# Prompt tokens read a second time channel by channel: the two front norms of a streaming encoder layer without transposes, and the first value products on unscaled channels

## The chip, the cores and the metric

The kernel runs on one core of one Trainium2 chip. The metric is device microseconds of one execution. A core has five engines that run their own instruction streams in order: TensorE (PE in the profile, with its weight loads as PEld), VectorE (DVE), ScalarE (ACT), GpSimd (POOL) and SyncE (SP, which here only issues DMAs). They wait for each other by semaphores.

## The reference

One layer is computed for 2048 prompt tokens and 32 sample tokens, with 1024 channels. What matters here is its start; everything behind it is unchanged.

```python
def rmsnorm(x, g):
    xf = x.astype(jnp.float32)
    y = xf * lax.rsqrt(jnp.mean(xf * xf, axis=-1, keepdims=True) + EPS)
    return (y * g.astype(jnp.float32)).astype(x.dtype)

def layer(x, pool_hist, n_valid, S0, g_pre_mix, w_in, ...):
    h = rmsnorm(x, g_pre_mix)
    z = h @ w_in
    u, zq, zf, zi, zg = jnp.split(z, [...], axis=-1)   # 512 columns each
    ...                      # pooling mixer on u, HGRN2 recurrence on q, f, i, g
    y_mix = jnp.concatenate([y_pool, y_hg], axis=-1) @ w_out
    x = x + rmsnorm(y_mix, g_post_mix)
    h2 = rmsnorm(x, g_pre_ffn)
    f = (jax.nn.silu(h2 @ w_gate) * (h2 @ w_up)) @ w_down
    return x + rmsnorm(f, g_post_ffn), ...
```

The norm's root belongs to a token, its gain g to a channel. The columns zi are the "values" of the recurrence: values = h @ w_in[:, 1536:2048].

## The kernel before

**Halves and stages.** The prompt is worked in two halves A and B of 1024 tokens, B together with the sample tokens. Each half goes through the same stages: front (norm, channels onto partitions), values, four heads (products f, q, g and the recurrence), four pooling groups, output projection, second norm, gate and up. At the end one down projection serves both halves. Half B's front starts while half A's last gate/up products run (`gate_up(S, on_last)` calls it eleven steps before its end).

**Precision.** Every large product is made of three products of rounded f32 values: an operand is split into a high part (a copy that rounds, on ACT) and a low part (operand minus high part, on DVE), and high x high, high x low and low x high are summed in PSUM. `split` does that for weights (tiles whw, wlw or whi, wlo), and hThi, hTlo hold the normed activations.

**The front.** `front_norm(S, tg)` treats a group of 512 tokens (tg 0 or 1). It loads four tiles xt of 128 tokens x 1024 channels, sums their squares on ACT (`sumsq`, tile junk), forms the roots on POOL (`rstd_of`), scales the tiles on DVE, and `to_channels` transposes them on PE into PSUM banks tps, 128x128 at a time, 32 transposes per group. Out of PSUM, ACT writes hThi with the gain as its scale, and DVE writes hTlo. At the program's start the first 256 tokens go ahead of the rest, and the vectors of gains (tile rows) are transposed by PE into vec.

**The values.** `values(S, tg)` takes eight rows of w_in in pairs and makes, for four token tiles and each channel row k, three products 128x512 into four PSUM banks (vps). In half A the first two pairs of tiles are worked apart, since their channels come at different times. Then come the heads. `head_products` makes f for tokens 0 to 511 and 512 to 1023, then q for both, then g.

**Order.** PE's order is the order in which the program is written; generator tasks (`Task`, `poll`) are stepped in between by a counted time of PE. The other engines' orders, SP's queue among them, are made by a scheduler. Weights come through `Stream`: `want` lists the loads, `ahead(n)` issues loads two items beyond n and splits the items up to n, `take` hands out the next. Large SBUF tiles come from a pool of 39 buffers (UP), tiles of 512 columns from one of 22 (TP), PSUM from two pools of four banks (MM for the large products, AX for everything else).

Of the kernel before, what the change touches and what calls it, by code (L numbers as in the profile page):

```python
# [16 lines left out]
P = 128  # L17
D = 1024
# [25 lines left out]
C_END = C_I4 + NS  # L44
# [29 lines left out]
def body(tc, ins, outs, cst):  # L74
    nc = tc.nc
    ctx = ExitStack()
    with ctx:
# [28 lines left out]
        x_first = []  # L106
        rows = t2("rows", [32, P])
        nc.vector.memset(rows, 0.0)
        for i in range(2):
            xt = ztile("xt", [P, D])  # L110
            nc.sync.dma_start(out=xt, in_=ins["x_prompt"][0, i * P:(i + 1) * P, :])
            x_first.append((xt, P))
            if i == 0:
                nc.sync.dma_start(out=cons, in_=cst)
            else:
                for ap, r0, n in ((ins["g_pre_mix"], 0, 8), (ins["g_pre_ffn"], 8, 8), (ins["pool_scale"], 16, 4),
                                  (ins["lb_logits"], 20, 8), (ins["g_hg_norm"], 28, 1)):
                    nc.sync.dma_start(out=rows[r0:r0 + n, :], in_=ap.rearrange("a (k p) -> (a k) p", p=P))
        ident = cons[:, C_ID:C_ID + P]
        x_p = ins["x_prompt"][0]  # L120
        x_s = ins["x_sample"][0]
        w_in = ins["w_in"][0]
# [5 lines left out]
        vec = CP.tile([P, 32], F32, name="vec")  # L128
        vps = axbank("vps")
        nc.tensor.transpose(vps[:, 0:32], rows, ident[0:32, 0:32])  # L130
        nc.vector.tensor_copy(vec, vps[:, 0:32])
# [16 lines left out]
        nc.gpsimd.memset(nhalf, -0.5)  # L148
        wpool = CP.tile([P, 4, P], F32, name="wpool")
# [88 lines left out]
        def raw_rows2(w, k, c0):  # L238
            raw = ztile("wrow", [P, 2 * 512])
            nc.sync.dma_start(out=raw.rearrange("p (k c) -> p k c", c=512),  # L240
                              in_=w[k * P:(k + 2) * P, c0:c0 + 512].rearrange("(k p) c -> p k c", p=P))
            return raw
# [11 lines left out]

        def ahead(n):
            its = Stream.items
            while Stream.nraw < min(n + LOOKRAW, len(its)):
                its[Stream.nraw] = its[Stream.nraw]()
                Stream.nraw += 1
# [43 lines left out]

        tcB = [0]

        def to_channels(tiles, dst, gcol, col0, seen=None, which=()):
            n = P * len(tiles)
            per = 512 // n
            for k0 in range(0, KD, per):
                ps = axbank("tps")  # L310
                for kk in range(per):
                    for i, xn in enumerate(tiles):
                        c = kk * n + i * P
                        nc.tensor.transpose(ps[:, c:c + P], xn[:, (k0 + kk) * P:(k0 + kk + 1) * P], ident)
                        tick(107)
                for kk in range(per):
                    k = k0 + kk
                    src = ps[:, kk * n:(kk + 1) * n]
                    hi, lo = dst[k]
                    nc.scalar.activation(hi[:, col0:col0 + n], src, AF.Copy, scale=gcol[:, k:k + 1])  # L320
                    nc.vector.scalar_tensor_tensor(lo[:, col0:col0 + n], src, gcol[:, k:k + 1],
                                                   hi[:, col0:col0 + n].bitcast(F32), ALU.mult, ALU.subtract)
                if seen is not None:
                    for i in which:
                        seen[i] = k0 + per
                yield (700.0 if seen is None and tcB[0] else 400.0) * per
# [95 lines left out]
        def make_half(B):  # L422
            S = Half()
            S.B = B
            S.T = TMAX if B else HALF
            S.tok0 = HALF if B else 0
            S.blocks = [(0, 512), (512, 1024)]
            return S


        def front_norm(S, tg):
            def channels():
                if S.hT is None:
                    S.hT = [(xtile(f"hThi{k}"), xtile(f"hTlo{k}")) for k in range(KD)]
                    if S.B:
                        S.hsr = SP.tile([P, KD, NS], F32, tag="hs", name="hsr", bufs=1)
                        S.ysr = SP.tile([P, KD, NS], F32, tag="ysr", name="ysr", bufs=1)

            early = not S.B and tg == 0
            xs = list(x_first) if early else []  # L440
            if early:
                ahead(0)
            for i in range(len(xs), 4):
                xt = ztile("xt", [P, D])
                r0 = S.tok0 + (tg * 4 + i) * P
                nc.sync.dma_start(out=xt, in_=x_p[r0:r0 + P, :])
                xs.append((xt, P))
            if S.B and tg == 1:
                xq = ztile("xts", [NS, D])
                nc.sync.dma_start(out=xq, in_=x_s)  # L450
                xs.append((xq, NS))
            yield 1000.0 if S.B else 0.0
            if early:
                channels()
                for a in (0, 2):
                    for xt, r in xs[a:a + 2]:
                        st = new_stat()
                        sumsq(xt, r, st[0:r, 0:1])
                        nc.vector.tensor_scalar(xt, xt, rstd_of(st, r, eng=nc.vector), None, ALU.mult)
                    yield 2000.0  # L460
                    yield from to_channels([x for x, _ in xs[a:a + 2]], S.hT, g_pre, a * P, S.seen[tg], (a // 2,))
                return
            rs = []
            for xt, r in xs:
                st = new_stat()
                sumsq(xt, r, st[0:r, 0:1])
                rs.append(rstd_of(st, r))
            for (xt, r), q in zip(xs, rs):
                nc.vector.tensor_scalar(xt, xt, q, None, ALU.mult)
            xq = xs[4][0] if len(xs) > 4 else None  # L470
            xs = [x for x, _ in xs[:4]]
            yield 8000.0 if S.B else 6000.0
            channels()
            yield from to_channels(xs, S.hT, g_pre, tg * 512, S.seen[tg], (0, 1))
            if xq is not None:
# [3 lines left out]
        def front_loads(S):  # L479
            for tg in range(2):  # L480
                for k in range(0, KD, 2):
                    want(lambda k=k: raw_rows2(w_in, k, COL_I), 1 if S.B or tg else 2)
# [10 lines left out]
        def values(S, tg):  # L493
            va, vb = ztile("va", [P, 2, 512]), ztile("vb", [P, 2, 512])
            S.vt += [va[:, 0], va[:, 1], vb[:, 0], vb[:, 1]]
            smp = S.B and tg == 1
            pss = [mmbank("vps") for _ in range(4)]
            sps = axbank("vsps") if smp else None
            four = Four(sps, KD)
            early = not S.B and tg == 0  # L500
            ws = {}
            steps = [(k, (0, 1, 2, 3)) for k in range(0, KD, 2)]
            if early:
                steps[0:2] = [(0, (0, 1)), (2, (0, 1)), (0, (2, 3)), (2, (2, 3))]
            for k, tiles in steps:
                if k not in ws:
                    ws[k] = take(1 if early else 2)
# [1063 lines left out]
```

## Time and profile before

| what | us |
|---|---|
| median of 3 runs (lowest to highest) | 2188.99 (2187.97 to 2190.52) |
| the profiled execution | 2187.68 |
| its span | 2185.9 |
| PE idle in the span | 42.2 |
| first transposes of xt | 9.1 |
| first value product | 14.34 |
| head 0's first product | 70.67 |
| first transposes of half B | 818.3 |
| its values begin | 841.5 |

The span runs from the first to the last instruction that the profiler records. Busy shares are of the span. A matmul's duration overlaps with that of the next, so on PE the step between two starts is what one costs. Durations of a group are means of one instruction in ns. The rows in the chapter on the prediction are copied from the profile's views as they are.

### The profile page before, as it was taken

How to read it: one execution, taken by the hardware profiler on the slowest of the kernel's cores; microseconds unless marked ns; L12 is line 12 of the kernel's file. 1: busy time of each engine (PE TensorE's matmuls, PEld its weight loads, DVE VectorE, ACT ScalarE, POOL GpSimd, SP SyncE). 2: the span in 40 equal slices, each digit the busy share in tenths (PEclk: the TensorE clock that was granted, in tenths of full speed). 3: DMA queues.
4: the chain of work that ended last, by engine and by line, in shares of the span. 5: the costliest groups of instructions: out<-in, count | busy, mean ns of one | idle time of the engine just before them, and what ended most of it. 6: DMA issues, size and time to landing. Idle time of an engine off the chain costs nothing.

```text
span 2185.9 us, 34308 instructions
## 1 busy us (share of the span) xinstructions
PE 2143.7 (98%) x13293; PEld 1712.5 (78%) x13293; DVE 1414.3 (65%) x2309; ACT 817.5 (37%) x1586; POOL 282.4 (13%) x383
## 2 busy tenths in 40 slices
PE   7999999999999999999999999999999999999996
PEld 5878878788888888777777778888888777877785
DVE  6356665697776778365574687766666756566585
ACT  6233234554444456132323564444444521011032
POOL 1033201100000001023220120000000210110033
PEclk9999999999999999999999999999999999999999
DMA  6110043425555558111014524544454797777789
GB/s 221 39 31 21 21 145 131 149 82 169 162 148 151 155 164 268 43 44 34 15 32 146 180 86 125 159 141 140 135 145 140 228 327 200 220 223 206 203 226 308
DMA packets 385179, 315.13 MB, mean 144 GB/s; under 512 B 15701, under 2 KB 318058, under 8 KB 385017
## 3 DMA queue, kind: packets, MB, share of 16 engines
q1 hardware_dynamic: 382856, 305.34, 46.0%
q0 software_dynamic: 2016, 7.34, 1.7%
q8 instruction: 105, 1.72, 0.3%
q14 instruction: 58, 0.47, 0.1%
q10 hardware_dynamic: 144, 0.26, 0.0%
HBM read 214.51 MB, written 98.37 MB: 143 GB/s over the span
## 4 chain that ended last, share of the span: by engine, by line
PE 43%; DVE 3%; DMA 2%; ACT 1%; POOL 1%; issue 0%; SPq 0%; DVEq 0%; POOLq 0%; ACTq 0%
PE gx L184 10%; PE dx L184 10%; PE gy L184 6%; PE dy L184 5%; PE ops L184 4%; PE dz L184 2%; PE gz L184 2%; PE mmb L184 1%; DMA hst<-hdTrue 1%; PE gsps L184 1%; DVE acc L1360 1%; PE gw L184 1%; PE sacc L184 0%; PE zps L184 0%; PE pps L184 0%
## 5 line engine op out<-in xcount | busy, mean ns | idle before, releaser
L184 PE MATMUL gx<-fhi,wf 128*128 128x512 f32 x1376 | 448.5, 394 | 0.0
L184 PEld LDWEIGHTS gx<-fhi,wf 128*128 128x128 f32 x1376 | 258.7, 188 | 59.2 <-issue 1.0
L184 PE MATMUL gx<-flo,wf 128*128 128x512 f32 x688 | 270.1, 393 | 0.0
L184 PE MATMUL gy<-fhi,wf 128*128 128x512 f32 x704 | 234.0, 394 | 0.0
L184 PE MATMUL mmb<-hThi,whi 128*128 128x512 f32 x512 | 219.0, 428 | 0.0
L184 PE MATMUL dx<-dhi,hst 128*128 128x512 f32 x640 | 213.5, 394 | 0.5 <-DVE acc L1360 0.4
L184 PE MATMUL mmb<-hThi,wlo 128*128 128x512 f32 x512 | 201.4, 393 | 0.0
L184 PE MATMUL mmb<-hTlo,whi 128*128 128x512 f32 x512 | 201.2, 393 | 0.0
L1360 DVE TENSOR_TENSOR acc<-dx,acc 128x512 f32<-128x512 f32 x168 | 115.2, 689 | 77.9 <-PE dx L184 77.3
L1094 DVE TENSOR_TENSOR wf<-s,wf 128x512 fp32r<-128x512 f32 x176 | 120.5, 688 | 66.1 <-ACT wf L1089 63.5
L184 PEld LDWEIGHTS gy<-fhi,wf 128*128 128x128 f32 x704 | 132.3, 188 | 30.6 <-issue 0.5
L184 PEld LDWEIGHTS gx<-flo,wf 128*128 128x128 f32 x688 | 129.6, 188 | 28.3
L1089 ACT CAST wf<-s 128x512 fp32r<-128x512 f32 x176 | 108.4, 621 | 105.4 <-PE gy L184 34.7
L184 PEld LDWEIGHTS dx<-dhi,hst 128*128 128x128 f32 x640 | 120.8, 189 | 32.2 <-issue 3.6
L184 PE MATMUL gy<-flo,wf 128*128 128x512 f32 x352 | 138.2, 392 | 0.0
L184 PE MATMUL dx<-dlo,hst 128*128 128x512 f32 x320 | 125.9, 394 | 0.0
L1094 DVE TENSOR_TENSOR wf<-wraw,wf 128x512 fp32r<-128x512 f32 x132 | 89.7, 687 | 50.9 <-ACT wf L1089 50.8
L184 PE MATMUL dy<-dhi,hst 128*128 128x512 f32 x320 | 113.1, 394 | 4.8 <-DMA hst<-hdTrue 4.4
L184 PEld LDWEIGHTS mmb<-hThi,whi 128*128 128x128 f32 x512 | 96.3, 188 | 25.0 <-issue 6.4
L1089 ACT CAST wf<-wraw 128x512 fp32r<-128x512 f32 x132 | 80.9, 620 | 88.3 <-PE gz L184 23.8
L184 PEld LDWEIGHTS mmb<-hThi,wlo 128*128 128x128 f32 x512 | 96.1, 188 | 22.3
L184 PEld LDWEIGHTS mmb<-hTlo,whi 128*128 128x128 f32 x512 | 96.7, 189 | 18.3 <-issue 2.6
(312 smaller groups left out, 4115.1 us busy)
## 6 DMA issues: line engine op xcount, KB each, us to landing
hst<-hdFalse SPq DMA_DIRECT2D x140, 256.0 KB, 2.9
hst<-hdTrue SPq DMA_DIRECT2D x140, 256.0 KB, 3.4
wraw<-in_w_gate_dram SPq DMA_DIRECT2D x50, 512.0 KB, 4.0
wraw<-in_w_up_dram SPq DMA_DIRECT2D x50, 512.0 KB, 3.9
hdFalse<-hhi SPq DMA_DIRECT2D x77, 256.0 KB, 2.6
hdFalse<-hlo SPq DMA_DIRECT2D x77, 256.0 KB, 2.5
hdTrue<-hhi SPq DMA_DIRECT2D x77, 256.0 KB, 2.4
hdTrue<-hlo SPq DMA_DIRECT2D x77, 256.0 KB, 3.1
```

The lines of the kernel that those rows point to most:

```text
L184: nc.tensor.matmul(out, l, r, start=start, stop=stop, skip_group_check=more)
L1089: nc.scalar.copy(wf[:, 0], getattr(M, src) if isinstance(src, str) else src)
L1094: nc.vector.tensor_tensor(wf[:, 1], getattr(M, src) if isinstance(src, str) else src, wf[:, 0].bitcast(F32), ALU.subtract)
L1360: nc.vector.tensor_tensor(dst, ps, dst, ALU.add)
```

## The change

The host hands the prompt over a second time, transposed (`x_channels`, 1024 channels x 2048 tokens), and puts the vectors of gains and bounds into 32 columns of the table of constants. The transposes of the front go.

- A group's channels are loaded directly: tiles xT, two channel rows of 128 partitions x 512 tokens each.
- The roots are still summed from token tiles (`token_stats`, half A) or from half rows of them (`later_stats`, half B, a task in half A's head stage, with its own loads xtl and 16 Squares). POOL multiplies the unit matrix by a tile's roots (dg), and four products of a matrix of ones with dg spread the 512 roots over all partitions of a PSUM bank rb.
- `scaled_channels` then forms x * g * rb on DVE, in place in xT, copies it to hThi on ACT and subtracts to hTlo on DVE.
- Half A starts with `first_values`, which replaces its front and its two value stages. There all engines follow the written order. The first group's products use channels scaled with the gain alone (tiles xg, split into high and low); the roots, a factor per token, are multiplied into the finished values (ACT and DVE, two tiles each). The second group's products use hThi and hTlo as before. The first group's hThi and hTlo are made at the end.
- Half A's head 0 makes f and q for tokens 512 to 1023 first, then f and q for tokens 0 to 511; the other heads and the pooling take the blocks in that order too.

The vectors come by one DMA on ACT's queue, the shape constants by one on SP's behind the first channels and weights; the five small loads of rows, their transpose and their copy go.

```diff
-        x_first = []
-        rows = t2("rows", [32, P])
...
+        nc.scalar.dma_start(out=cons[:, C_VEC:C_END], in_=cst[:, C_VEC:C_END])
...
-        nc.tensor.transpose(vps[:, 0:32], rows, ident[0:32, 0:32])
-        nc.vector.tensor_copy(vec, vps[:, 0:32])
+        vec = cons[:, C_VEC:C_END]
...
-        def to_channels(tiles, dst, gcol, col0, seen=None, which=()):
...
+        def channel_load(S, tg, k, n):
+            t0 = S.tok0 + tg * 512
+            nc.sync.dma_start(out=S.xT[tg][k // 2][:, k % 2:k % 2 + n], in_=x_t[:, k:k + n, t0:t0 + 512])
...
+        def token_stats(S, tg):
+
+            S.rs[tg], S.dg[tg] = [], t2("dg", [P, 4, P])
+            for i, xt in enumerate(S.xt[tg]):
+                st = new_stat()
+                sumsq(xt, P, st[:, 0:1])
+                S.rs[tg].append(rstd_of(st, P))
+                nc.gpsimd.tensor_scalar(S.dg[tg][:, i], ident, S.rs[tg][i], None, ALU.mult)
...
+        def later_stats(S):
+
+            st = S.st
+            for i in range(NCH):
+                for c in range(2):
+                    x = t2("xtl")
+                    r0 = S.tok0 + i * P
+                    nc.sync.dma_start(out=x, in_=x_p[r0:r0 + P, c * 512:c * 512 + 512])
+                    sumsq(x, P, st[:, 2 * i + c:2 * i + c + 1])
+                    del x
+                yield 20000.0
...
+        def scaled_channels(S, tg):
+            rb = axbank("rb")
+            for i in range(4):
+                mm(rb[:, i * P:(i + 1) * P], ones, S.dg[tg][:, i], True, True, 112.0)
...
+            for k in range(0, KD, 2):
+                x = S.xT[tg][k // 2]
+                for i in range(2):
+                    nc.vector.scalar_tensor_tensor(x[:, i], x[:, i], g_pre[:, k + i:k + i + 1], rb, ALU.mult, ALU.mult)
+                    nc.scalar.copy(S.hT[k + i][0][:, cs], x[:, i])
+                for i in range(2):
+                    hi, lo = (t[:, cs] for t in S.hT[k + i])
+                    nc.vector.tensor_tensor(lo, x[:, i], hi.bitcast(F32), ALU.subtract)
...
+        def first_values(S):
+
+
+            front_loads(S)
+            S.xT[0] = [ztile("xT", [P, 2, 512]) for _ in range(4)]
+            for kp in range(4):
+                channel_load(S, 0, 2 * kp, 2 if kp else 1)
+                raws(kp + 1)
+                if kp == 0:
+                    channel_load(S, 0, 1, 1)
+            nc.sync.dma_start(out=cons[:, 0:C_VEC], in_=cst[:, 0:C_VEC])
...
+            token_tiles(S, 1)
...
+            token_tiles(S, 0)
+            unscaled(0)
+            ahead(1)
+            unscaled(1)
+            pss = value_tiles(S)
+            for k in range(0, KD, 2):
+                _, hi, lo = take(0)
+                if k + 2 < KD:
+                    unscaled(k + 2)
+                    ahead(Stream.used + 1)
+                    unscaled(k + 3)
...
+                if k == 4:
+                    token_stats(S, 1)
+                for kk in range(2):
+                    ah, al = xg.pop(k + kk)
+                    for i in range(4):
+                        value_products(pss, i, ah, al, i * P, hi[kk], lo[kk], k + kk == 0, k + kk == KD - 1)
+                    if k + kk == KD - 3:
+                        later = scaled_channels(S, 1)
+                        next(later)
+                        next(later)
...
+        with tc.manual_schedule(engines=set(mybir.EngineType) - {mybir.EngineType.Unassigned}):
+            first_values(halves[0])
...
+    arrays["x_channels"] = np.ascontiguousarray(inputs["x_prompt"][0].T)
```

**PE at the program's start.** Before, after its branch, PE begins like this (vps in the first row is the bank of the transposed vectors, tps those of the tokens):

```order
L130 MATMUL vps<-cons,rows 128x32
L314 MATMUL tps<-cons,xt 128x128 x4
L184 MATMUL vps<-whw,hThi_116 128x512
L184 MATMUL vps<-wlw,hThi_116 128x512
L184 MATMUL vps<-whw,hTlo_117 128x512
L314 MATMUL tps<-cons,xt 128x128 x4
```

Now it begins with value products on xg, and around the first rb group, behind 72 of them, stand these rows:

```order
L173 MATMUL vps<-wlw,xg 128x512
L173 MATMUL vps<-whw,xg 128x512
L173 MATMUL rb<-dg,ones 128x128 x4
L173 MATMUL vps<-whw,xg 128x512
L173 MATMUL vps<-wlw,xg 128x512
```

So no transposes stand among the value products, and 24 products of the first group of tokens follow the spreading of the second group's roots.

**ACT at the program's start.** Its first rows were a table load and Squares of xt; now they are, with what each waits for:

```order
L107 DMA cons<-shape_constants 128x32
L527 ACT_TABLE_LOAD [waits DMAHW1_49]
L527 ACTIVATE xg<-xT,cons 128x512 [waits DMAHW0_49]
L210 CAST whw<-wrow 128x512 [waits DMAHW2_49]
L210 CAST whw<-wrow 128x512 [waits DMAHW3_49]
L527 ACTIVATE xg<-xT,cons 128x512 [waits DMAHW4_49]
```

DMAHW0, 2, 3 and 4 are the first loads on SP's queue, DMAHW1 the load in the first row. The table load, which waited for nothing before, now stands behind the landing of the vectors.

**DVE around the first rb.** These are its rows from the last split of the first value stage on:

```order
L211 TENSOR_TENSOR wlw<-wrow,whw 128x512 x2
L528 SCALAR_TENSOR_TENSOR xg<-xT,cons,xg 128x512
L455 SCALAR_TENSOR_TENSOR xT<-xT,cons,rb 128x512 x2
L459 TENSOR_TENSOR hTlo_303<-xT,hThi_302 128x512
L459 TENSOR_TENSOR hTlo_305<-xT,hThi_304 128x512
L211 TENSOR_TENSOR wlw<-wrow,whw 128x1024
L560 COPY va<-vps 128x512
```

Before, a pair of channel rows for 512 tokens took DVE two rows (hTlo from PSUM) and the tiles' scaling by roots; now it takes four, and the split of the second stage's weights and the copies of the first stage's values stand between the pairs.

More of the change, by code (lines that the diff above doesn't have):

```diff
@@ L426, in make_half, with channel_tiles @@
             S.tok0 = HALF if B else 0
-            S.blocks = [(0, 512), (512, 1024)]
+            S.blocks = [(0, 512), (512, 1024)] if B else [(512, 1024), (0, 512)]
             return S
[L431 to L444, printed above, removed]
+        def channel_tiles(S, tg):
+            S.xT[tg] = [ztile("xT", [P, 2, 512]) for _ in range(4)]
+            for k in range(KD):
+                channel_load(S, tg, k, 2 - k % 2) if k % 2 == 0 else None
@@ L452, in front_norm @@
[L452 to L462, printed above, removed]
```

240 lines of the change are left out of this document (138 added, 102 removed).

## The prediction

> **What bounds the kernel now.** I read the page first, then the waits of PE, then the busy time by stretches, then the timeline of PE at the places that the change touches. In the stretches, the columns are the stretch in us, its length, the busy time of PE, PEld, DVE, ACT and POOL with counts, the granted clock, the DMA share and GB/s.
>
> ```profile
> span 2185.9 us, 34308 instructions
> PE 2143.7 (98%) x13293; PEld 1712.5 (78%) x13293; DVE 1414.3 (65%) x2309; ACT 817.5 (37%) x1586; POOL 282.4 (13%) x383
> ...
> PE vps L130 <- DMA rows<-in_g_hg_norm_dram: 8.1, 1, 8.1
> ...
> 0.00:71.00 71.00, 56.09 (x263) 44.62 (x264) 35.80 (x68) 35.03 (x63) 8.25 (x22) 1.00 0.59 193
> 71.00:800.00 729.00, 725.12 (x4637) 587.46 (x4636) 488.94 (x801) 310.87 (x611) 78.76 (x116) 1.00 0.37 110
> 800.00:865.00 65.00, 65.00 (x320) 52.82 (x319) 51.30 (x75) 42.27 (x70) 9.80 (x18) 1.00 0.77 244
> ```
>
> TensorE bounds it. Of the 42.2 us in which PE is idle, 14.9 lie in the first 71 us; the 65 us in which the second half's front is made have none. So an edit pays only by taking instructions off PE or by closing that first hole. The program's order on PE, compared before and after, differs only in the first values stage and around 815 to 865 us; the head, projection, gate/up and down stages keep their instructions in their order. I therefore count two places and let the rest shift as a block.
>
> **The front, as it is.** These rows are PE's timeline (start, duration, instruction); the step between starts, not the duration, is what a matmul costs.
>
> ```profile
> 14.34 0.79 PE L184 MATMUL vps<-whw,hThi 128*128 128x512 f32 x1 [3.15 <-ACT whw L221]
> ...
> 16.04 0.79 PE L184 MATMUL vps<-wlw,hThi 128*128 128x512 f32 x1 [0.91 <-DVE wlw L222]
> 16.63 0.63 PE L184 MATMUL vps<-whw,hTlo 128*128 128x512 f32 x1
> 17.06 1.05 PE L314 MATMUL tps<-cons,xt 128*128 128x128 f32 x4
> ...
> 18.77 0.62 PE L184 MATMUL vps<-whw,hTlo 128*128 128x512 f32 x1
> 19.19 0.63 PE L314 MATMUL tps<-cons,xt 128*128 128x128 f32 x4
> ...
> 48.05 0.42 PE L164 MATMUL cps<-cons,cachet 15*128 15x15 f32 x4
> 48.40 0.50 PE L184 MATMUL vps<-whw,hThi 128*128 128x512 f32 x1
> ...
> 70.67 0.39 PE L184 MATMUL mmb<-hThi,whi 128*128 128x512 f32 x1
> ```
>
> The first value product starts at 14.34 and head 0's f product, the first work that the change leaves alone, at 70.67. From 48.40 to 70.67 stand 96 value products: 0.232 each. In the first 3.2 us from 16.04 on the step is 0.43 (16.63 to 17.06, 18.77 to 19.19), although the granted clock is shown as 1.00.
>
> ```profile
> 852.53 0.60 PE L314 MATMUL tps<-cons,xt 128*128 128x128 f32 x4
> 852.89 0.48 PE L184 MATMUL vps<-whw,hThi 128*128 128x512 f32 x1
> 853.20 0.39 PE L184 MATMUL vps<-wlw,hThi 128*128 128x512 f32 x1
> 853.43 0.39 PE L184 MATMUL vps<-whw,hTlo 128*128 128x512 f32 x1
> 853.66 0.60 PE L314 MATMUL tps<-cons,xt 128*128 128x128 f32 x4
> ...
> 136.13 0.38 PE L184 MATMUL ops<-va,attn 128*128 128x128 f32 x2
> ...
> 137.83 0.48 PE L184 MATMUL mmb<-hThi,whi 128*128 128x512 f32 x1
> ```
>
> One group of four transposes and three products takes 853.66 - 852.53 = 1.13, less 3 x 0.23 is 0.44 for the four transposes. There are 16 groups per half. The new products with ones are plain f32, 128x128; the nearest row is the 16 f32 products of that shape from 136.13 to 137.83: 0.106 each, 0.43 for four. Bounds: not below 0.43, not above four steps of a 512-wide product, 0.93. I take 0.43.
>
> **When the first product can start.** Rows, from the timeline, from the groups of the first 70 us and from the list of DMA issues (size, us to landing):
>
> ```profile
> 0.73 1.28 ACT L288 ACT_TABLE_LOAD   x1 [0.73 <-PEq L1549]
> 4.41 1.06 ACT L288 ACTIVATE junk<-xt 128x1024 bf16<-128x1024 f32 x1 [2.40 <-DMA xt<-in_x_prompt_dram]
> 5.37 0.19 ACT L288 ACTIVATION_READ_ACCUMULATOR junk<-xt 128x1 f32 x1
> ...
> S<-in_state_hgrn_dram SPq DMA_DIRECT2D x4, 64.0 KB, 1.9
> ...
> L321 DVE SCALAR_TENSOR_TENSOR hTlo<-tps,vec,hThi 128x512 fp32r<-128x512 f32 x8 | 6.0, 750 | 2.3 <-ACT hThi L320 2.3
> L320 ACT ACTIVATE hThi<-tps,vec 128x512 fp32r<-128x512 f32 x8 | 5.5, 689 | 5.1 <-PE tps L314 5.1
> L222 DVE TENSOR_TENSOR wlw<-wrow,whw 128x512 fp32r<-128x512 f32 x8 | 5.2, 685 | 0.0
> L295 POOL TENSOR_TENSOR st<-st,nhalf 128x1 f32<-128x1 f32 x8 | 4.9, 608 | 15.3 <-DVE st L294 14.9
> L222 DVE TENSOR_TENSOR wlw<-wrow,whw 128x1024 fp32r<-128x1024 f32 x4 | 4.7, 1214 | 0.0
> L221 ACT CAST whw<-wrow 128x512 fp32r<-128x512 f32 x8 | 4.5, 617 | 0.0
> L294 POOL TENSOR_SCALAR st<-st 128x1 f32<-128x1 f32 x4 | 1.3, 318 | 14.5 <-ACT junk L288 14.5
> L592 POOL MEMSET cmp<- 128x128 f32 x2 | 0.9, 480 | 0.0
> ...
> L636 POOL TENSOR_TENSOR k_t<-k_t,tt 128x512 f32<-128x512 f32 x5 | 7.0, 1403 | 7.2 <-issue 5.8 <-PE lv L184 1.3
> ```
>
> Now ACT fetches the 16 KB of vectors itself at about 0.8 and, as its order shows, its table load waits for them. A 64 KB load lands in 1.9; the 512 KB of xt, ready for ACT at 4.41 after an issue at 0.73, are the other end. I take 1.9: landed at 2.7, table loaded (1.28) at 4.0. The 256 KB of the first channel tile and of the first half weight row are there by then or within 0.4. Then one ACTIVATE (0.69) and one CAST (0.62): first product at **5.4** (by the other end 7.1). VectorE makes the low parts, 0.75 and 0.69, so the second product waits 0.4.
>
> **Sum of the front.** 5.4, plus 0.4, plus 192 x 0.232 = 44.5, plus slow steps: for 3.4 us one product per 0.43 instead of 0.232, 3.4 x (1 - 0.232/0.43) = 1.6 (bounds: none, and the 4.85 us from 14.34 to 19.19, 2.2), plus two groups with ones, 0.9, plus the four cache transposes, 48.05 to 48.40 in the old order, 0.35. That is 53.2 for head 0's f product in place of 70.67: **-17.5 us**. The pieces of before agree: 9 us later start, 6.6 for 15 transpose groups, the rest waits.
>
> The Trainium skill ("TensorE: Matmul & The Clock Gate", section "What's actually happening") says that the array's clock is gated to half until a free-running window of about 3.4 us has been busy, and again after an idle one. The trace agrees with the half rate (0.43 against 0.232), and its slow stretch is 3.2 us long from 16.04; by the rule, since the window is free-running, the stretch could be nearly twice as long, an estimate of up to 1.8 us more on the sum.
>
> **What could hold PE inside the front.** Three places have no old counterpart. All these engines now run in written order.
>
> ```profile
> 0.00:10.00 10.00, 0.76 (x2) 0.36 (x2) 1.75 (x6) 3.58 (x5) 1.92 (x8) 1.00 0.78 272
> 10.00:20.00 10.00, 5.65 (x19) 4.02 (x20) 6.80 (x20) 6.08 (x13) 1.10 (x2) 1.00 1.02 375
> ```
>
> (a) The first rb group, after 72 products, needs the root of every token of tiles 4 to 7. Ahead of and with them stand 2.10 MB of channels, 2.10 of weights, 0.18 of constants and 2.10 of tokens: 6.47 MB. The kernel before brought 2.72 + 3.75 = 6.47 MB in its first 20.0 us, at a full DMA share in the second half. Last Square 1.25, then POOL 0.32 + 0.61 and the scaled unit matrix (between 0.48, the row of that shape, and the 1.4 of its 128x512 products; 0.48 taken): 22.7. PE comes there at 5.4 + 0.4 + 1.6 + 72 x 0.232 = 24.1. Covered by 1.4.
>
> (b) The second rb group, before the last 12 products, needs four Squares on ACT that stand behind the last weight split of the second value stage, which follows VectorE: four channel pairs of 2 x 0.75 + 2 x 0.685 + 1.21 = 4.1, and two copies, 17.7 after the first rb at 24.5, so 42.2; Squares 5.0, POOL 1.4: 48.6. PE arrives at 24.5 + 108 x 0.232 = 49.6. Covered by 1.0, and a tenth more on every vector and scalar instruction uses that up and costs 1 to 2.
>
> (c) The first 512 channels-by-token block is scaled last, on VectorE from about 53.5, 8 x 1.44 = 11.5 plus some 2 of other work: 67. Its products now come second (f and q of the other block first, 48 x 0.232): the eighth k is needed at 69.2. Covered by 2.
>
> The second half's Squares, now 16 of half a row each in the head stage, with their loads, lie beside PE: ACT is busy 311 of the 729 us from 71 to 800. Their DMAs stand in SP's queue between weight loads that are fetched three items, 33 us of products, ahead. I cost them at nothing; without that cover, up to 15 us.
>
> **The second half's front.** 16 transpose groups go, 7.0, two groups with ones come, 0.9: **-6.2 us** on PE, which has no idle time there. VectorE gains 8 x 0.685 and loses 4 x 0.75 per tile group, +2.5.
>
> ```profile
> 850.00:860.00 10.00, 10.00 (x60) 8.41 (x59) 9.56 (x14) 8.24 (x13) 2.41 (x4) 1.00 1.11 362
> 860.00:870.00 10.00, 10.00 (x52) 8.05 (x51) 7.31 (x11) 5.95 (x10) 0.00 (x0) 1.00 0.80 228
> ```
>
> At 850 to 860 it is 96% busy, but the second group's pairs are wanted one per 24 products (5.6 us), until about 875, and the next 10 us have 2.7 idle. I cost it at nothing; uncovered, 2.5.
>
> **Sum.** -17.5 - 6.2 = -23.7. The profiled execution took 2187.68 (its span 2185.9 and 1.8 around it), so 2164.0; the median of the runs is 1.3 above it, so **2165.3** for a median.
>
> **Rivals.**
> 1. DMA feeds (a) too late. For it: if the rate stays at the 272 GB/s of the first ten us, 6.47 MB take 23.8, the rb group is ready at 26.5 and costs 2.4; 2 KB pieces of x_channels are new. Two such waits, and slow steps again after them: 2168 to 2174. Against: the 375 of the second ten us, in which w_in too came in 2 KB pieces. 14%.
> 2. The wait moves to the chain of (b), or to 850 to 870: 2167 to 2171. 15%.
> 3. The slow steps last twice the 3.4 us that I count: 1.6 more, 2167. 6%.
> 4. A Square in the head stage stands on ACT ahead of a sigmoid while its load hangs in SP's queue behind a buffer. For it: SP already waits there,
>
> ```profile
> SPq L235 <- DVE state L752: 66.8, 3, 36.6
> ```
>
> and four PSUM banks let PE run on for 4 x 5.5 = 22 us: the longest wait would cost 14.6, so 2180. Against: in the order each of these loads waits only for work that stands well ahead of its Square. 4%.
> 5. Slower than before: DMA starves the whole front. The second rb group needs 12.8 MB: the channels, weights and tokens of both groups, and constants. After the last token tile come 1.25 + 1.4 + 0.43 + 12 x 0.232 + 0.35 = 6.2, so f starts at 12.8/r + 6.2. At r = 0.16 MB/us that is 86, +33 against 53, and with the -23.7 about 2198. It decides from r = 0.18 down, where the whole gain is gone; the two windows above have 0.27, with its slow start, and 0.38. 2%.
> 6. More than forecast, by small stalls that I left in (up to 4 us): 2161. 4%.
>
> **How the numbers follow.** The forecast, 2163 to 2167, has 55%. The range, 2160.5 to 2174, takes in case 6 and cases 1 to 3 and leaves out cases 4 and 5 and tails. A measurement of this kernel tells 0.2%, 4.4 us, from no change. Faster by more than that: all but 4 and 5 and some odd mishap, 96%; within it 2%; slower 2%.
>
> **What would show it.** PE's first product near 5.4 and head 0's first at 53; no wait of rb for dg above 1 us; 16 products of rb in place of 128 transposes of xt, and no idle PE from 780 to 850; the head stage as long as before. Wrong would be: rb waiting on a DMA-released Square (case 1) or on POOL after ACT's last four Squares (case 2), PE idle on sg or a sigmoid around 60 to 300 (case 4).

## The result, and the profile after

The changed kernel takes 2171.54 us (median of four runs, 2170.91 to 2172.42), the kernel before 2189.76 (four runs beside them, 2187.97 to 2190.73): a ratio of 0.9917, with a 95% interval from 0.9904 to 0.9931, so 18.2 us less. The forecast was 23.7 less: 2165.3, in a range from 2160.5 to 2174.0. The direction and both places were right, and the measured gain is about three quarters of the forecast one. The profiled executions differ by 16.8 (2187.68 and 2170.91).

The page of the changed kernel, its first rows, and the list of what PE waited for (total, times, longest), first of the kernel before, then of the changed one:

```profile
span 2169.1 us, 34220 instructions
...
PE 2133.7 (98%) x13196; PEld 1702.3 (78%) x13196; DVE 1425.6 (66%) x2321; ACT 823.2 (38%) x1604; POOL 288.4 (13%) x391
```

```profile
PE vps L184 <- ACT whw L221: 3.1, 1, 3.1
...
PE tps L314 <- DVE xt L459: 1.5, 2, 0.8
```

```profile
PE vps L173 <- ACT whw L210: 7.3, 1, 7.3
...
PE rb L173 <- POOL dg L424: 1.1, 1, 1.1
```

PE works 10.0 us less than before (2143.7) and is idle for 35.4 in place of 42.2. PE's waits for tiles to transpose are gone. Its idle time ahead of the first value product fell from 12.7 (8.1 for the rows, shown with the prediction, 1.5 and 3.1) to 7.3, and one wait is new: rb on POOL's dg.

Busy time by stretches, cut at events that both kernels have: head 0's first product, the first gate/up product, half B's first product on sample tokens (head 0), the first and the last down product. First of the kernel before, then of the changed one (columns as in the prediction):

```profile
0.00:70.67 70.67, 55.76 (x261) 44.33 (x262) 35.67 (x67) 34.72 (x62) 8.25 (x22) 1.00 0.59 194
...
407.40:892.20 484.80, 484.58 (x2165) 393.17 (x2167) 356.51 (x546) 238.31 (x412) 17.61 (x34) 1.00 0.54 160
...
1725.60:2174.50 448.90, 441.38 (x1937) 348.97 (x1936) 278.97 (x389) 81.58 (x141) 77.22 (x81) 1.00 0.81 239
```

```profile
0.00:57.37 57.37, 48.90 (x212) 39.36 (x213) 33.45 (x55) 35.16 (x58) 14.00 (x33) 1.00 0.82 294
...
395.00:874.10 479.10, 479.03 (x2117) 388.60 (x2119) 360.22 (x554) 229.04 (x396) 14.96 (x26) 1.00 0.54 162
...
1706.70:2157.20 450.50, 443.64 (x1936) 348.94 (x1935) 279.31 (x389) 81.55 (x141) 77.48 (x82) 1.00 0.80 238
```

The lengths of all stretches, with a second profile of each kernel from the experiments below (e4 and e0):

| stretch up to | before (two profiles) | changed (two profiles) | its variants |
|---|---|---|---|
| head 0's first product | 70.7, 71.4 | 57.4, 57.3 | edited, see below |
| first gate/up product | 336.7, 336.3 | 337.6, 337.3 | 335.0 to 336.8 (e6 edits it) |
| half B's first sample product | 484.8, 485.3 | 479.1, 479.6 | 478.6 to 480.0 (e7 edits it) |
| first down product | 833.5, 834.3 | 832.6, 833.4 | 832.2 to 834.8 |
| last down product | 448.9, 448.6 | 450.5, 451.6 | 449.1 to 451.1 |

The front gave 13.3 to 14.1, half B's front 5.7: 19 to 20. The stages between them keep their lengths within their scatter of 1 to 2 us. Only the down stage is longer each time; this is taken up below.

Now the front, from PE's timeline (start, duration, instruction, and in brackets the idle time ahead and who ended it):

```profile
7.26 0.79 PE L173 MATMUL vps<-whw,xg 128*128 128x512 f32 x1 [7.26 <-ACT whw L210]
...
10.02 1.06 PE L173 MATMUL vps<-whw,xg 128*128 128x512 f32 x2
...
11.26 0.63 PE L173 MATMUL vps<-whw,xg 128*128 128x512 f32 x2
...
26.00 1.05 PE L173 MATMUL rb<-dg,ones 128*128 128x128 f32 x8
26.81 0.47 PE L173 MATMUL vps<-whw,xg 128*128 128x512 f32 x1
...
51.92 0.83 PE L173 MATMUL rb<-dg,ones 128*128 128x128 f32 x6
53.87 0.49 PE L173 MATMUL rb<-dg,ones 128*128 128x128 f32 x2 [1.12 <-POOL dg L424]
54.11 0.48 PE L173 MATMUL vps<-whw,hThi 128*128 128x512 f32 x1
...
57.37 0.50 PE L173 MATMUL mmb<-hThi,whi 128*128 128x512 f32 x1
```

Three numbers stand beside the forecast's. The first product comes at 7.26, not 5.4. A group of four products with ones takes 26.81 - 26.00 = 0.81, not 0.43, and shows as eight records: each f32 product leaves two. The second group takes 54.11 - 51.92 = 2.19, so it is held for 1.38, of which the profile shows 1.12 as idle time, where no wait was expected. The reason for the first, from ACT's timeline and from the list of DMA issues (size, us to landing):

```profile
0.73 0.41 ACTq L107 DMA_DIRECT2D cons<-shape_constants  x1
4.69 1.28 ACT L527 ACT_TABLE_LOAD   x1 [4.69 <-DMA xT<-x_channels]
5.98 0.72 ACT L527 ACTIVATE xg<-xT,cons 128x512 fp32r<-128x512 f32 x1
...
49.08 0.19 ACT L283 ACTIVATION_READ_ACCUMULATOR junk<-xt 128x1 f32 x1
```

```profile
cons<-shape_constants ACTq DMA_DIRECT2D x1, 16.0 KB, 4.1
```

The 16 KB of vectors took 4.1 to land, like the 256 KB pieces that were issued with them (4.2). By ACT's order the table load stood behind the vectors. The bracket of its row names the channels, whose load was issued at the same time and landed at nearly the same time. The reason for the third, from POOL's and from DVE's timeline:

```profile
23.61 0.61 POOL L424 TENSOR_SCALAR dg<-cons,st 128x128 f32<-128x128 f32 x1
...
46.75 0.61 POOL L424 TENSOR_SCALAR dg<-cons,st 128x128 f32<-128x128 f32 x1
...
48.39 0.61 POOL L424 TENSOR_SCALAR dg<-cons,st 128x128 f32<-128x128 f32 x1
...
50.03 1.15 POOL L424 TENSOR_SCALAR dg<-cons,st 128x128 f32<-128x128 f32 x1
...
52.40 1.41 POOL L424 TENSOR_SCALAR dg<-cons,st 128x128 f32<-128x128 f32 x1
```

```profile
50.08 1.39 DVE L217 TENSOR_TENSOR wlo<-wraw,whi 128x512 fp32r<-128x512 f32 x2
51.40 0.48 DVE L574 TENSOR_SCALAR va<-va,st 128x512 f32<-128x512 f32 x1
52.33 0.49 DVE L574 TENSOR_SCALAR vb<-vb,st 128x512 f32<-128x512 f32 x1 [0.46 <-POOL st L290]
52.73 1.38 DVE L217 TENSOR_TENSOR wlo<-wraw,whi 128x512 fp32r<-128x512 f32 x2
```

The first row ends the first group's chain, at 24.22. In the second, POOL needs 1.64 per tile (46.75 to 48.39) where ACT delivers a Square every 1.18, and its last two unit matrices take twice as long as the first two. It ends 4.5 us after ACT's last Square (49.27 to 53.81), not 1.4.

### The profile page after: what moved, and what is told of

Its sections match the earlier page's. It is cut to its first block, busy times and chain, and to the rows that moved or that the text cites. A ratio compares the mean times of both kernels' runs of the same rounds, so it can differ in the third digit from the quotient of the medians.

```text
span 2169.1 us, 34220 instructions
## 1 busy us (share of the span) xinstructions
PE 2133.7 (98%) x13196; PEld 1702.3 (78%) x13196; DVE 1425.6 (66%) x2321; ACT 823.2 (38%) x1604; POOL 288.4 (13%) x391
## 4 chain that ended last, share of the span: by engine, by line
PE 88%; DVE 4%; ACT 2%; DMA 1%; issue 1%; POOL 1%; DVEq 0%; POOLq 0%; SPq 0%; ACTq 0%
PE gx L173 21%; PE mmb L173 16%; PE gy L173 11%; PE dx L173 9%; PE ops L173 9%; PE dy L173 5%; PE gz L173 5%; PE dz L173 2%; PE vps L173 2%; PE gb L173 1%; DMA hst<-hdTrue 1%; PE gw L173 1%; PE gsps L173 1%; PE ups L173 1%; DVE acc L1447 1%
```

## Experiments

Each edit is made to the changed kernel, except for e4. Ratios are to the kernel before, run on the same chip. f is head 0's first product.

| run | edit | us, median (lowest to highest) | ratio, 95% interval | first product | f |
|---|---|---|---|---|---|
| e0 | none | 2171.51 (2169.98 to 2173.26) | 0.9913, 0.9899 to 0.9926 | 7.20 | 57.27 |
| e1 | table load early | 2171.61 (2171.25 to 2172.45) | 0.9914, 0.9900 to 0.9927 | 5.73 | 56.61 |
| e2 | Squares early | 2171.20 (2169.03 to 2173.06) | 0.9911, 0.9897 to 0.9924 | 7.09 | 56.55 |
| e3 | PE kept busy | 2170.19 (2169.45 to 2173.04) | 0.9909, 0.9895 to 0.9922 | 6.70 | 55.42 |
| e4 | (kernel before) | 2190.22 (2188.07 to 2192.21) | 1.0003, 0.9994 to 1.0011 | - | 71.4 |
| e5 | e1 + e2 + e3 | 2166.79 (2165.56 to 2167.94) | 0.9893, 0.9880 to 0.9907 | 6.13 | 54.27 |
| e6 | old order in the heads | 2179.16 (2177.53 to 2179.99) | 0.9948, 0.9934 to 0.9962 | 7.20 | 60.18 |
| e7 | products with ones twice | 2173.95 (2173.64 to 2177.57) | 0.9930, 0.9918 to 0.9943 | 7.13 | 58.15 |
| e8 | weight split later | 2170.54 (2168.68 to 2172.41) | 0.9914, 0.9901 to 0.9928 | 7.23 | 57.55 |
| e9 | e5 + tokens early | 2165.45 (2163.91 to 2166.81) | 0.9888, 0.9875 to 0.9902 | 5.97 | 53.33 |

The runs e0 to e3 stood on one chip and e4 to e9 on another. The medians of the kernel before were 2191.01 on the first, and 2189.62 (e4 to e7) and 2190.51 (e8, e9) on the second, so times are compared across the two only to about 1 us.

Differences of 1 us between two of these medians are within their scatter, so e1, e2, e3 and e8 are read from f and from their traces.

**e0: the changed kernel again.**

> The changed kernel as it is, once more, as the measure for the others of this chip. Two questions. First, how far its stages repeat: from the last gate/up product to the last down product it took 450.5 us in the profile after the change and 448.9 before, with the same instructions. If that is scatter between executions, this run lands anywhere from 448.5 to 451; if the change costs something there, it shows 450 to 451 again. Second, the three sizes that the forecast had wrong at the front: first product at 7.26 (not 5.4), 0.81 per group of four products with ones (not 0.43), a wait of 1.12 in front of the second such group. They should come back within 0.1. Time 2171.5.

7.20, 0.81, a wait of 1.11, f at 57.27: the three sizes come back. The down stage took 451.6.

**e1: the table load ahead of the vectors.**

```diff
+            warm = CP.tile([P, 4], F32, name="warm")
+            nc.scalar.activation(warm, nhalf, AF.Copy)
             front_loads(S)
```

> One small copy on ScalarE, from a constant that needs no DMA, stands ahead of the first activation, so that the table load comes before the landing of the vectors. Theory: the table load (1.28) stands behind the vectors' landing at 4.69 and is all that can be saved; the first product moves from 7.26 to about 6.0, and everything behind follows, since the roots' chain starts from the same products: head 0's first product at 56.1 in place of 57.4, the time 2170.3. Rival A: DMA feeds the first activations, so the table load was hidden in part: first product at 6.5 or later. Rival B: the second group with ones waits for roots that are bound by DMA and POOL, so its wait grows by what the start gains (1.1 to 2.4) and head 0 stays at 57.4.

The first product came 1.5 earlier: 1.28 is the table load, and the rest came from loads that landed a little earlier in this execution (the vectors after 3.7, in e0 after 4.0). ACT's timeline of e1 shows what then bounds the start, the landing itself:

```profile
4.45 0.72 ACT L529 ACTIVATE xg<-xT,cons 128x512 fp32r<-128x512 f32 x1 [1.79 <-DMA cons<-shape_constants]
```

But f came only 0.66 earlier. PE's timeline of e1 shows where the rest stayed:

```profile
5.73 0.80 PE L173 MATMUL vps<-whw,xg 128*128 128x512 f32 x1 [5.73 <-ACT whw L210]
...
11.04 0.80 PE L173 MATMUL vps<-whw,xg 128*128 128x512 f32 x2
11.69 0.39 PE L173 MATMUL vps<-wlw,xg 128*128 128x512 f32 x1
```

The step of 0.43 lasts until 11.3 or so, as in the changed kernel, though it begins 1.5 earlier. Each us of it costs 1 - 0.232/0.43 = 0.46, so 1.7 more of it give back 0.8. That loss belongs to this execution and not to the edit as far as the runs show, since the end of the slow steps scatters among executions that begin them at the same time (see below). Neither rival holds: the table load was not hidden, and the second group's wait stayed 1.12.

**e2: Squares of the first tokens in ACT's holes.**

```diff
                 ahead(Stream.used + 1)
-                if k == 2:
+                if k == 0:
+                    token_stats(S, 0, (0,))
+                elif k == 2:
+                    token_stats(S, 0, (1,))
                     next(later, 0)
                 elif k == 4:
-                    token_stats(S, 0)
+                    token_stats(S, 0, (2, 3))
```

> The Squares of the first group of tokens come one each in the two holes of 2.0 us that ScalarE has between the second stage's channel pairs, and two where four stood. Theory: the wait of 1.12 (1.4 with the refill) in front of the second group with ones is the end of the chain of four Squares and POOL's roots and scaled unit matrices; two of them earlier, POOL ends about 48.5 and the wait goes: head 0's first product at 56.0, time 2170.2. Rival: POOL's own operations set it, 0.61 for a scaled unit matrix while VectorE is idle and 1.15 to 1.41 while it works; with the Squares put beside VectorE's work all of them get slow and the wait stays, or the Squares hold up the copies of hThi and the value products wait: 57.4 or later.

PE's timeline of e2, around the second group:

```profile
52.46 1.05 PE L173 MATMUL rb<-dg,ones 128*128 128x128 f32 x8
53.26 0.47 PE L173 MATMUL vps<-whw,hThi 128*128 128x512 f32 x1
```

The wait is gone: one piece of 0.80. f came 0.72 earlier, not 1.3, because here too the slow steps lasted longer, to about 12.8. POOL ended at 50.55, two us later than expected: about 1.0 of that is its last power and unit matrix, which again stood beside DVE's work (1.09 and 1.04 in place of 0.57 and 0.61), and 0.7 the slow steps ahead (the first group with ones came at 26.57, in e0 at 25.89). 1.9 of cover were left.

**e3: TensorE kept busy from 1.0 on.**

```diff
+            wm = axbank("wm")
+            for i in range(12):
+                mm(wm[:, 0:P], ones, ones, True, True, 0.0)
             front_loads(S)
```

> Twelve products of ones with ones into a bank that nobody reads, ahead of the first value product, while TensorE waits for it. Theory: the first 8 value products step at 0.43 in place of 0.232 because TensorE was idle before; kept busy for some 5 us, it runs at full step from its first product at 7.26 on, and head 0's first product comes 1.3 to 1.7 earlier: 55.7 to 56.1, time 2170.0. Rival A: the slow steps are the supply of the low parts by VectorE: steps stay 0.43 and nothing is won. Rival B: the gain is taken back in the second group with ones, whose roots do not come earlier: its wait grows by 1.5 and head 0 stays at 57.4.

PE's timeline of e3:

```profile
1.02 5.30 PE L173 MATMUL wm<-ones 128*128 128x128 f32 x24 [1.02 <-POOL cmps L142]
6.70 0.50 PE L173 MATMUL vps<-whw,xg 128*128 128x512 f32 x1 [0.37 <-ACT whw L210]
...
7.91 0.62 PE L173 MATMUL vps<-whw,xg 128*128 128x512 f32 x2
8.38 0.39 PE L173 MATMUL vps<-wlw,xg 128*128 128x512 f32 x1
```

Two products take 0.47 from 7.91 on: the slow steps are gone, and f comes 1.85 earlier (0.5 of it because the first product did: the loads landed that much earlier in this execution, the vectors after 3.5, in e0 after 4.0). So the slow steps were TensorE's own and not DVE's supply. Rival B falls too: the second group's wait stayed 1.12 while all of it moved forward, so its roots follow from the same products.

**e4: the kernel before, again.**

> The kernel before, unchanged, profiled a second time, to tell scatter from cost. Compared by stages with the profile of before: front to head 0's first product 70.67; from the first product of half B's sample tokens in head 0 back to there, and the down stage (first to last product of it 448.9; in four profiles of the changed kernel and its variants 450.4 to 451.6). Theory: the 1.6 us that the changed kernel seems to lose in the down stage, and 1 to 2 us between 350 and 1700, are scatter of stages that the change leaves alone; this run shows 449 to 451.5 in the down stage. Rival: the change costs 1.5 us there, and this run shows 448.9 within 0.3 again. Time about 2190.

448.6: the rival's number. The ten profiles of the changed kernel and its variants have 449.1 to 451.6, the two of before 448.9 and 448.6. That speaks against scatter, and PE's steps in that stage, given below under what stays open, do so more clearly.

**e5: the three edits together.**

> The early table load, the twelve warming products and the earlier Squares together. By theory the three are not a plain sum: the warming products end at about 6.3 and hold the first value product to there (5.7 with the table load alone); the slow steps go; the first roots become the bound, since POOL ended their last scaled unit matrix at 24.6 when only the table load came earlier, 0.4 later than in the changed kernel, so the first group with ones waits about 1 from 23.6; the wait of the second group is gone. Head 0's first product at 24.6 + 0.81 + 108 x 0.232 + 0.81 + 12 x 0.232 + 0.35 = 54.4, 2.9 earlier than in the changed kernel run again; time 2168.6. Rival: the first roots come by DMA no later than in the changed kernel (24.2 or before) and the gains add: 53.5, 2167.7. Other rival: earlier products only meet slower supplies, 55.4 as with the warming products alone.

PE's timeline of e5, around the first group:

```profile
23.32 0.83 PE L173 MATMUL rb<-dg,ones 128*128 128x128 f32 x6
24.84 0.49 PE L173 MATMUL rb<-dg,ones 128*128 128x128 f32 x2 [0.69 <-POOL dg L425]
```

f at 54.27, 0.1 from the sum, with the wait in the place that was named: the first group was covered only because PE came late. The time is 4.7 below that of e0, and the runs of the two don't overlap; they stood on different chips, and by the ratios to the kernel before the gain is about 4.4, with intervals that overlap a little. The trace is the firmer evidence.

**e6: the heads' old order of blocks.**

```diff
-            S.blocks = [(0, 512), (512, 1024)] if B else [(512, 1024), (0, 512)]
+            S.blocks = [(0, 512), (512, 1024)]
...
-            if h == 0 and not S.B:
+            if h == 0 and False:
```

> Head 0 of the first half makes its products in the old order again (f for tokens 0 to 511 first), and so do the other heads and the pooling. Theory: the channels of the first 512 tokens are finished by VectorE one pair after the other until about 70, and the new order is what hides it; now TensorE waits at 57.4, 59, 62 and 64 for pairs that come at about 60.5, 63.6, 66.3 and 70.0, and the block ends at 71.4 in place of 63: 8.4 later, time 2180. Rival: VectorE, with no other head work to do at that time, finishes the pairs at its bare rate of 2.9 each from 57.7, the last at 69.2, and TensorE finds other work in the program: less than 4 later.

7.7 later than e0, 8.4 expected. PE's timeline of e6 at the first and the last pair of channels:

```profile
60.18 0.49 PE L173 MATMUL mmb<-hThi,whi 128*128 128x512 f32 x1 [1.74 <-ACT hThi L456]
...
68.27 0.50 PE L173 MATMUL mmb<-hThi,whi 128*128 128x512 f32 x1 [0.53 <-ACT hThi L456]
```

PE takes the pairs as DVE finishes them, every 2.7 or so. By the profiles the first gate/up product comes 7.4 later than in e0, and 1.1 of that lies ahead of head 0, where the slow steps lasted longer (the first group with ones came at 27.02, in e0 at 25.89). So the new order hides some 6 to 8 us.

**e7: the products with ones made twice.**

```diff
-                mm(rb[:, i * P:(i + 1) * P], ones, S.dg[tg][:, i], True, True, 112.0)
+                for _ in range(2):
+                    mm(rb[:, i * P:(i + 1) * P], ones, S.dg[tg][:, i], True, True, 112.0)
```

> Each of the 16 products with ones is made twice, into the same place. Theory: a group of four costs 0.81 on TensorE, since each f32 product of 128 columns shows as two records of 0.1 each, and not the 0.43 of the forecast. Three groups then cost 0.81 more each; in the group that waits for its last unit matrix three of four pairs fit into the wait, so it costs 0.2 to 0.8 more: 2.6 to 3.2 in all, time 2174.3, head 0's first product at 58.3 to 58.9. Rival: 0.43 a group, 1.3 to 1.7 in all, 2173.

2.4 more than e0 by the medians. The trace is more exact; PE's timeline of e7:

```profile
25.68 1.95 PE L173 MATMUL rb<-dg,ones 128*128 128x128 f32 x16
27.38 0.47 PE L173 MATMUL vps<-whw,xg 128*128 128x512 f32 x1
```

Eight products take 1.70, 0.21 each, and half B's front took 480.8, 1.2 to 1.7 more, for two groups. 0.81 a group holds, 0.43 falls.

**e8: VectorE out of POOL's way.**

```diff
-                ahead(Stream.used + 1)
+                if k < 6:
+                    ahead(Stream.used + 1)
...
+            ahead(Stream.used + 1)
             for i in range(4):
                 (nc.vector.tensor_copy if i % 2 else nc.scalar.copy)(S.vt[4 + i], pss[i])
```

> The changed kernel, but ScalarE and VectorE split head 0's first weight tile after the second group with ones instead of beside POOL's last roots; the Squares stand where they stood. Theory: the last two scaled unit matrices took 1.15 and 1.41 in place of 0.61, and their powers 0.69 in place of 0.57, because VectorE's subtractions and multiplications from SBUF stood beside them; with VectorE nearly empty there, both take 0.61 to 0.9, POOL ends 0.8 to 1.3 earlier, and the wait of 1.1 in front of the second group with ones goes to 0 to 0.3. Head 0's first product at 56.2 to 56.5, unless the later split holds it up. Rival: POOL is slow there for another cause (ScalarE's accesses, its own position in the program): 1.15 and 1.41 again, the wait stays.

Half of it came. POOL's timeline of e8:

```profile
50.73 0.81 POOL L424 TENSOR_SCALAR dg<-cons,st 128x128 f32<-128x128 f32 x1
...
52.57 1.41 POOL L424 TENSOR_SCALAR dg<-cons,st 128x128 f32<-128x128 f32 x1
```

The third unit matrix fell from 1.15 to 0.81, with one large DVE instruction beside it, a scaling of 0.60, and the power behind it from 0.69 to 0.57; the wait fell from 1.11 to 0.57. But f came at 57.55 and not at 56.2 to 56.5: the slow steps lasted 5.6 in this execution (3.9 in e0), which cost 0.8. The last one met DVE's split after all and took 1.41. The edit doesn't separate DVE from the place in the program for that one; e9 does.

**e9: token tiles of the second group ahead of the last channels.**

```diff
             for kp in range(4):
+                if kp == 3:
+                    nc.sync.dma_start(out=cons[:, 0:C_VEC], in_=cst[:, 0:C_VEC])
+                    token_tiles(S, 1)
                 channel_load(S, 0, 2 * kp, 2 if kp else 1)
...
-                if k == 4:
+                if k == 2:
                     token_stats(S, 1)
```

> As with the three edits together, and the token tiles of the second group are loaded ahead of the last pair of channels and weights, their Squares one value step earlier on ScalarE. Theory: the first group with ones waited 0.7 (0.9 with the refill) for roots whose Squares stood behind the landing of the token tiles; now they come 2 to 3 earlier and TensorE is not held: head 0's first product at 53.4, 0.9 earlier than with the three, time 2166. Rival: the last pair of channels and weights comes too late in its turn, or ScalarE's Squares hold up its split: the value products wait as much, 54.3 or later.

PE's timeline of e9:

```profile
23.30 1.05 PE L173 MATMUL rb<-dg,ones 128*128 128x128 f32 x8
24.11 0.48 PE L173 MATMUL vps<-whw,xg 128*128 128x512 f32 x1
...
53.33 0.50 PE L173 MATMUL mmb<-hThi,whi 128*128 128x512 f32 x1
```

No wait, f at 53.33, 0.1 from the sum. At 2165.45 this is the fastest version, 6 us below e0, which ran on the other chip. It also answers e8: here the first group's last unit matrix, which took 0.61 beside an idle DVE in the changed kernel, meets DVE's weight split (L211, 20.97 to 22.26). POOL's timeline of e9:

```profile
19.20 0.61 POOL L425 TENSOR_SCALAR dg<-cons,st 128x128 f32<-128x128 f32 x1
...
21.26 1.40 POOL L425 TENSOR_SCALAR dg<-cons,st 128x128 f32<-128x128 f32 x1
```

So it isn't the place in the program. Nor is it ScalarE: in the changed kernel the matrix at 48.39 stood beside a Square of ACT for its whole length and took 0.61, and so did the one of e2 at 38.90, beside a cast of ACT for most of its length.

## Why the prediction was right, and where its size was off

**What bounds, and where.** Right. The gain lies in the two places that were counted, and the stages between them kept their lengths within 1 us. Only the down stage grew, by 1.7.

**When the first product can start: 5.4, measured 7.26.** The mechanism was right, the table load behind the vectors (e1), and the far end of the bounds, 7.1, was passed by 0.2. The term that failed is the landing, taken as 1.9 from a 64 KB load of a quiet moment. The vectors took 4.1, as long as the 256 KB loads beside them, and this put the table load, 1.28, into the chain. The first channels, expected by 4.0 or within 0.4, were late as well: ACT's row has them as the last to land, at 4.69, so that even with the vectors in time the first product would have come at about 6.0. Cost at f: 1.9, of which 1.3 hang on the vectors and 0.6 on the channels.

**Slow steps: 1.6, measured 1.7 here, but not a constant.** That the size came out is in part luck: the 3.4 us that the sum counts stand in no row (the row shown has 3.2), and the stretch differs between executions. The step of 0.43 began at 7.1 to 7.3 in six profiles and ended between 10.7 (e7) and 13.6 (e6), so it lasted 3.6 to 6.4 us; this alone moves f by 1.3. Case 3, twice the 3.4 us counted, happened in part, in some executions and not in others. (The prediction prices that case at 1.6 and, in another place, at 1.8; 3.4 x 0.46 is 1.6.) The Trainium skill ("TensorE: Matmul & The Clock Gate", section "What's actually happening") has it so: the window that is watched runs freely, so the slow stretch depends on where in it the first product falls. The spread from 3.6 to 6.4 agrees with that, though it is wider than the ±0.5 us by which, in that section, the point of change varies. No run shows the window itself. e3 shows that work ahead of the first product takes the stretch away.

**Two rb groups: 0.43 each, measured 0.81.** The row was misread: "16 f32 products" were 16 records, and each product leaves two. The upper bound, 0.93, held. Cost: 0.8 at f and 0.8 in half B's front.

**(a), the first rb group: covered by 1.4.** PE was not held: POOL ended at 24.2 and PE came at 26.0. But the roots were 1.5 later than forecast and the cover was a gift of the late start, as e5's wait of 0.7 shows. Case 1 did not occur.

**(b), the second rb group: covered by 1.0.** This fell, and case 2 came in its stead, at its place and with its price (1 to 2): 1.38. The term was POOL, 1.4 behind the last Square; it is 4.5, since POOL and not ACT is the slower link (1.64 against 1.18 a tile) and works at half speed beside DVE. The margin was said to vanish with a tenth more on every instruction; it was POOL's alone that took it. The prediction had named this sign of being wrong: rb waiting on POOL behind ACT's last four Squares.

**Sum of the front.** 53.2 was forecast for f, and it came at 57.37: 1.9 for the start, 0.8 for the groups, 1.4 for the wait and 0.1 for slow steps make 57.4. The first two are in none of the named cases. So the median lies above the forecast's own 2163 to 2167, and within the range to 2174 by the room that was left for cases 1 to 3, of which only case 2 came in full.

**(c), the first block:** right. Its last pair was done at 69.98 and wanted, counted from f at 57.37, at 72.7; e6 shows 6 to 8 us without the new order.

**The Squares of half B in the head stage at nothing:** right within scatter. That stretch took 337.6 and 337.3 against 336.7 and 336.3, but 335.0 to 336.8 in the variants, with the same Squares. Case 4 did not occur.

**Half B's front: -6.2, measured -5.7.** With 0.81 a group it is -5.4. PE still has no idle time there, so DVE's additional 2.5 was covered.

**What stays open.** The profiled execution was forecast at 2164.0 and took 2170.91. Of these 6.9 us the front explains 4.2, half B's front 0.5 and the down stage 1.7; the other stretches and the end of the span make up the rest, 0.5. (The medians are 6.2 apart, since the median lies 0.6 above the profiled execution and not 1.3.) The change leaves the down stage's instructions alone, and the prediction let it shift as a block. Its growth is no wait: PE's busy time rose, from 441.4 to 443.6 for the same number of products, while its waits fell a little. It is no scatter either. The mean step between two products of that stage (some 1800 steps, those from 0.215 to 0.26) is 0.2296 in both profiles of the kernel before, and 0.2309 to 0.2312 in all ten of the changed kernel and its variants; 1800 x 0.0014 are 2.5 us. In the other three stretches behind the front, the mean steps of the two kernels, each profiled twice, differ by 0.0002 at most. So the change brings it about. By what, where tiles come to lie or something else, was not tried.

## What to carry to other kernels

Where a stage is turned from "wait for everything" to "start with what is there", the gain is set by its chain of small steps. Here these were a 16 KB load issued beside large ones, a table load behind it, and the small operations of four tiles on the slowest engine of the chain. Price each link at the rate of its own engine, beside the work that will stand next to it, and count instructions rather than records. Covers of 1 us in such a chain were worth little: of the two here, one (1.0) was used up, and the other (1.4) held only by another delay.

## What the runs showed of the hardware

- A POOL operation on SBUF (128x128 f32, 0.61) took 1.15 to 1.41 beside DVE instructions that subtract two SBUF tensors. It took 0.81 beside one that scales a tensor (e8, at 50.73), and 1.04 beside two of these and short parts of two subtractions (e2, at 49.51). A 128x1 power took 1.09 in place of 0.57 beside such subtractions (e2, at 48.32) and 0.69 beside a scaling, but 0.57 again in e5 (at 45.98), where a subtraction ran beside most of it; what decides this no run shows. Beside DVE's scaling with rb, whose second operand lies in PSUM, the 128x128 operation took 0.61 (e2, at 38.9). The Trainium skill ("GPSIMD Engine Reference", section "1. Specifications") says that POOL shares its SBUF interfaces with VectorE and meets contention from instructions with two SBUF inputs or in a two-port mode. The subtractions agree, at a price of about a factor of two; whether the scaling runs in such a mode no run shows.
- The granted clock is shown as 1.00 in the first 20 us, though TensorE steps at 0.43 there for 3.6 to 6.4 us and at 0.232 behind twelve products that fill the idle time ahead (e3).
